# Moving the branch of an expert layer's overflow part from the end to behind the first expert

## The chip, the cores and the metric

One core of one Trainium2 chip runs the program. The metric is the device time of one execution in microseconds. The kernel before takes 1451.56 us (median of 3 runs, 1450.8 to 1453.4).

## The reference, cut to what matters

A decoder trunk of two layers on 256 tokens of width 1024. Each layer has a mixer of three kinds of heads, a feed-forward part and a gated input embedding; the first layer's feed-forward part is dense, the second's is a choice of two out of eight experts:

```
logits = t @ router;  top_val, top_idx = top_k(logits, 2);  gates = softmax(top_val)
for e in range(8):
    out = out + combine[:, e:e+1] * ((silu(t @ wg[e]) * (t @ wu[e])) @ wd[e])
h = h + out
h = h + sigmoid(rmsnorm(h) @ ple_gate) * (p @ ple_proj);   return rmsnorm(h)
```

Every expert has three float32 matrices of 1024 x 3584, 42 blocks of 1 MB; eight experts are 352 MB.

## The kernel before, in words

**Slots.** An expert's tokens are gathered into slots, multiplied, and added back into h. Expert 0 has 128 slots and is computed first, as a `Job`. The other seven are put in order of their number of tokens on the device; the three with fewest tokens get 64 slots each (`Halves`), the other four 128 (`Listed`). `ORDER` (L33) lists the places as they are worked on: 64, 128, 128, 64, 128, 128, 64 slots. Tokens past an expert's slots belong to the overflow part (`overflow`, L1181 to L1201): it loads the largest count into a register of every engine (L1183) and branches (L1184); only where some expert has too many tokens does a loop over all experts run (`Late`, two passes of a whole expert in its body). With the inputs used here the branch skips it.

**A cut.** An expert's 3584 columns are taken in cuts of 1024, 1024, 1024 and 512 (`run`, L1138). For a cut: `up` of the gate half, the transposes of the cut before (`turn`), `up` of the other half, `hidden` of the cut before, and `down` of the cut before. So the first cut of an expert stands ahead of the last `down` of the expert before it, and `scatter` (four adds into h, L1027) follows in the next steps. At the second cut of an expert the next one's rows are gathered and transposed (`prepare`), and the one after that is fetched by POOL (`fetch`, L1046).

**Arithmetic.** With 128 slots each block is split by ACT and DVE into a high part `whi` (L190) and a low part `wlo` (L191), and PE does 12 matmuls of 512 columns per block (L203). With 64 slots the blocks are used as they are, two blocks at a time in `up`, and the profile shows 8 matmul records of some 0.22 us per block.

**The ring.** All weight loads are issued by SP (`load`, L126), in the order of the program. A block goes into a buffer named raw. There are three pools: number 0 with 4 buffers, number 1 with 7, number 2 with 1. Unless a pool is named by `at`, `Ring.buffer` (L164) takes the one whose count of requests per buffer is lowest, and raises its count. The counts are kept by the program that writes the instructions, not by the chip, so they count what is written, run or not:

```
        def buffer(self, at=None):
            q = min(self.pools, key=lambda q: (q[2] + 1) / q[1]) if at is None else self.pools[at]
            q[2] += 1
            return q[0].tile([128, WMAX], FT, name="raw", tag="raw", bufs=q[1])
```

`Late` names pool 0 (L1036), and the last gate's weights name pool 1. A load waits until its buffer has been used up: with 128 slots when DVE has made `wlo`, with 64 when PE has done its matmuls.

**The end.** After the last expert's adds, `before_overflow` asks for the four blocks of the last gate (`ple_gate`, L656), then comes `overflow`, then `ple` (L662): h is transposed (L279), split (L230, L231), and multiplied with the gate's weights, which ACT and DVE scale and split (L195, L196); then the sigmoid, the last norm and the store. Nothing outside the branch's block is mixed with what is inside it, and no instruction crosses it.

Of the kernel before, what the change touches and what calls it, by code (L numbers as in the profile page):

```python
# [12 lines left out]
FR = mybir.dt.float32r  # L13
# [5 lines left out]
D = 1024  # L19
S = 256  # L20
NT = 2
KD = D // 128
# [75 lines left out]
def hymba_trunk(ctx: ExitStack, tc: tile.TileContext, A: dict, out: bass.AP, stop=None, dump=None):  # L98
# [14 lines left out]
    def aux():  # L113
        return psum.tile([128, 512], FT, name="aux", tag="aux")
# [10 lines left out]
    def load(t, src):  # L125
        nc.sync.dma_start(t, src)  # L126
        return t

    def const(name, p):
        lo, hi = _AT[name]  # L130
        C[name] = load(p.tile([128, hi - lo], FT, name="c_" + name), A["consts"][:, lo:hi])
        return C[name]
# [22 lines left out]
    class Ring:  # L155
        def __init__(self, p, raw, parts):
            self.p, self.parts = p, parts
            self.pools = [[p, raw, 0]]
# [70 lines left out]
    def split(hi, lo, src):  # L229
        ins = ACT.copy(hi, src)  # L230
        V.tensor_tensor(lo, src, hi.bitcast(FT), op=OP.subtract)  # L231
        return ins
# [654 lines left out]
        return xrow, slot, gate, rs, cmax_i, gates, places, who_i, slot_at, gate_at, caps, xd, rsd, rows_i  # L887


    def moe(ring, ep, slots, slots2, experts, routed, ready, before_overflow):  # L890
        xrow, slot, gate, rs, cmax_i, gates, places, who_i, slot_at, gate_at, caps, xd, rsd, rows_i = routed

        wg, wu, wd = A["moe_w_gate"][0], A["moe_w_up"][0], A["moe_w_down"][0]
# [6 lines left out]
        todo = []  # L900

        def step():
            if todo:
                todo.pop(0)()

        class Job:

            at = None
# [5 lines left out]
            def tiles(self):  # L914
                self.pe = ep.tile([128, NT, 128], FT, name="pe")
                self.pt = ep.tile([128, NT, 128], FR, name="pt")
                self.rs = ep.tile([128, 1], FT, name="rs_slot")

            def choose(self, names):
                for t in range(NT):  # L920
                    V.tensor_scalar(self.pe[:, t], names, self.col(t), None, op0=OP.is_equal)
# [19 lines left out]
            def prepare(self):  # L941

                self.tiles()
                xh, xl = (ep.tile([128, KD, 128], FR, name="xgh"), ep.tile([128, KD, 128], FR, name="xgl"))
                self.x = xh, xl

                def gather(k0):
                    ps = aux()
                    for j in range(4):
                        self.gathered(ps, j * 128, k0 + j, 128)  # L950
                    split(xh[:, k0:k0 + 4], xl[:, k0:k0 + 4], ps.rearrange("p (k n) -> p k n", k=4))

                return [lambda: self.choose(slots), lambda: gather(0), lambda: gather(4), self.scales, self.back]

            def unit(self, src, nk, n, pieces=1):
                return ring.unit(src, nk, n, pieces=pieces, halves=1, at=self.at)
# [77 lines left out]
        class Late(Job):  # L1034

            at = 0  # L1036

        class Listed(Job):

            names, n = slots, 128  # L1040
# [13 lines left out]
                PE.transpose(ps[:, at:at + self.n], self.xg[:self.n, k * 128:(k + 1) * 128], ident[:self.n, :self.n])  # L1054

            def prepare(self):
                xh, xl = (ep.tile([128, KD, 128], FR, name="xgh"), ep.tile([128, KD, 128], FR, name="xgl"))
                self.x = xh, xl

                def turn(k0):  # L1060
                    ps = aux()
                    for j in range(4):
                        self.turned(ps, j * 128, k0 + j)
                    split(xh[:, k0:k0 + 4], xl[:, k0:k0 + 4], ps.rearrange("p (k n) -> p k n", k=4))

                return [lambda: self.choose(self.names), lambda: turn(0), lambda: turn(4), self.back]

        class Halves(Listed):
# [5 lines left out]
            names, n = slots2, PCAP  # L1074
# [10 lines left out]
                return [lambda: self.choose(self.names), turn, self.back]  # L1085

            def unit(self, src, nk, n, pieces=1):
                return ring.fetch(src, nk, n, pieces)[0]

            def passes(self, os, x, ks, w, start, stop):  # L1090
                for n, o in enumerate(os):
# [43 lines left out]

        CUTS = [(c, min(1024, FE - c)) for c in range(0, FE, 1024)]

        def run(jobs, between=None):  # L1138

            steps = jobs[0].prepare()  # L1140
            for s in steps[:-1]:
                s()
            todo.append(steps[-1])
            if between:
                between()
            cuts = [(job, i) for job in range(len(jobs)) for i in range(len(CUTS))]
            back = None
            for cut in cuts + [None]:
                if cut:
                    job, (c0, n) = jobs[cut[0]], CUTS[cut[1]]  # L1150
                    pg = job.up(0, c0, n)
                if back:
                    pt = back[0].turn(back[3], back[2])
                if cut:
                    pu = job.up(1, c0, n)
                    with tc.issue_after(ring.split[0].ins):
                        job.gate_out(pg, n)
                if back:
                    with tc.issue_after(ring.split[0].ins), tc.issue_after(ring.split[1].ins):
                        hx = back[0].hidden(pt, back[2])  # L1160
                    us = back[0].down_units(back[1], back[2], 1 if cut else 2)
                if cut:
                    with tc.issue_after(ring.split[1].ins) if cut != cuts[-1] else nullcontext():
                        side = job.up_out(pu, n)
                if back:
                    back[0].down(back[1], hx, us)
                if cut:
                    back = (job, c0, n, side)
                    if cut[1] == 1 and cut[0] + 1 < len(jobs):
                        todo.extend(jobs[cut[0] + 1].prepare())  # L1170
                        if cut[0] + 2 < len(jobs):
                            todo.append(jobs[cut[0] + 2].fetch)
            while todo:
                step()

# [3 lines left out]
        se = ep.tile([128, NT, 2], FT, name="se", bufs=1)  # L1179

        def overflow():  # L1181
            V.memset(ei, 0.0)
            n_max = nc.values_load(cmax_i[0:1, 0:1], min_val=0, max_val=S + CAP - PCAP)  # L1183
            with tc.If(n_max > CAP):  # L1184
                xrow = ring.buffer(1)[:, :NT * D].rearrange("p (t d) -> p t d", t=NT)
                for t in range(NT):
                    load(xrow[:, t], xd[t * 128:(t + 1) * 128, :])
                for t in range(NT):
                    V.tensor_tensor(slot[:, t], slot[:, t], caps, op=OP.subtract)
                with tc.For_i(0, NE, 1) as e:  # L1190
                    V.tensor_scalar(hot, experts, ei, None, op0=OP.is_equal)
                    V.tensor_scalar(ei, ei, 1.0, None, op0=OP.add)
                    for t in range(NT):
                        for z, src in ((0, slot), (1, gate)):
                            hj = ep.tile([128, NE], FT, name="hj", bufs=2)
                            V.scalar_tensor_tensor(hj, hot, 1.0, src[:, t], op0=OP.mult, op1=OP.mult,
                                                   accum_out=se[:, t, z:z + 1])
                    for s0 in range(CAP, S + CAP - PCAP, 128):
                        sc = ep.tile([128, NT], FT, name="sc", bufs=2)
                        V.tensor_scalar(sc, se[:, :, 0], float(-s0), None, op0=OP.add)  # L1200
                        run([Late(lambda: e, lambda t: sc[:, t:t + 1], lambda t: se[:, t, 1:2], xrow)])  # L1201

        es = {}

# [7 lines left out]
        def between():  # L1212
            todo.append(know)
            todo.append(gates)

        jobs = ([Job(lambda: 0, lambda t: slot[:, t, 0:1], lambda t: gate[:, t, 0:1], xrow)]
                + [(Halves if j < NPACK else Listed)(j) for j in ORDER])
        run(jobs, between)
        before_overflow()
        overflow()  # L1220

    def store():
        for t in range(NT):
            nc.sync.dma_start(out[0, t * 128:(t + 1) * 128, :], h[:, t])

    ring = Ring(pool("ring"), 4, 3)
# [15 lines left out]
    with scoped("xt", 2, "right") as xp, scoped("xn", 2, "right") as xnp:  # L1242
# [47 lines left out]
        if stop == "mix1":  # L1290
# [4 lines left out]
        slots, below, experts, slots2, base, tok = [  # L1295
            const(n, pl) for n in ("slots", "below", "experts", "slots2", "base", "tok")]
# [15 lines left out]
        routed = routing(ring, pl, logits, g1, below, experts, base, tok, fill)  # L1312
    gates = []
    with scoped("moe", 2, "right") as ep, scoped("ringC", 1, "right") as rc:
        ring.widen(rc, 1)
        moe(ring, ep, slots, slots2, experts, routed, [first], lambda: gates.append(ple_gate(1, ring, 1)))
# [43 lines left out]
```

## Time and profile before

| | |
|---|---|
| median of 3 runs | 1451.56 us |
| profiled execution: time | 1452.36 us |
| its span, first to last instruction | 1450.6 us |
| mean granted TensorE clock in it | 0.992 |
| PE busy | 1398.5 us (96%) |
| DVE, ACT busy | 915.8 us (63%), 748.4 us (52%) |
| moved from HBM | 442.64 MB, 307 GB/s over the span |

The profile is that of one execution on the chip. Times count from the span's first instruction. PE is the matmul engine, PEld its weight loads, DVE, ACT, POOL and SP the other engines; a q behind an engine's name is its sequencer, which waits, branches and issues transfers. The DMA share is that of the 16 DMA engines. The expert layer begins near 500 us and ends at 1409 us.

### The profile page before, as it was taken

Reading aid. Unit: us, or ns where it says so; the run is one execution under the profiler, and the core shown is the slowest. Engines: PE = TensorE matmul, PEld = TensorE weight load, DVE = VectorE, ACT = ScalarE, POOL = GpSimd, SP = SyncE. Lnnn points to the kernel's source line nnn. Section 1 sums busy time; section 2 is a strip of 40 time slices with the busy share of each in tenths; the row PEclk is TensorE's granted clock in tenths of the full one; section 3 lists DMA queues with packets and bytes.
Section 4 is the critical chain, followed back from the end, with each engine's and each line's share of the span. In section 5 each row is a group of like instructions: output and inputs, shape, how many; then the busy total and the mean of one; then the engine's idle time right before and its main releaser. Section 6 shows DMA issues by size and latency. Waiting matters only on the chain. (4 is left out here: it accounts for less than half of the span.)

```text
span 1450.6 us, 19133 instructions
## 1 busy us (share of the span) xinstructions
PE 1398.5 (96%) x7330; PEld 1058.3 (73%) x7330; DVE 915.8 (63%) x1084; ACT 748.4 (52%) x874; POOL 69.0 (5%) x104
## 2 busy tenths in 40 slices
PE   8999999999999999999899999999999999999977
PEld 7987999997897887854378888864357888884426
DVE  6666555557766687831179898952158988882115
ACT  5455444447546566720167776741047767761006
POOL 0011000000001122000000000000000010000001
PEclk9999999999999999999999999999999999999998
DMA  8744555554634799999999999989999999999991
GB/s 287 207 145 138 176 194 183 183 195 148 223 117 148 194 307 366 403 408 409 401 409 399 402 408 409 385 338 382 402 408 409 389 408 409 402 376 356 371 363 45
DMA packets 168342, 446.09 MB, mean 308 GB/s; under 512 B 14449, under 2 KB 57713, under 8 KB 168242
## 3 DMA queue, kind: packets, MB, share of 16 engines
q1 hardware_dynamic: 166466, 440.83, 81.7%
q0 software_dynamic: 1776, 3.95, 1.2%
q8 instruction: 60, 0.98, 0.3%
q14 instruction: 40, 0.33, 0.1%
HBM read 442.64 MB, written 2.11 MB: 307 GB/s over the span
## 5 line engine op out<-in xcount | busy, mean ns | idle before, releaser
L191 DVE TENSOR_TENSOR wlo<-raw,whi 128x2048 fp32r<-128x2048 f32 (+2 forms) x348 | 638.3, 1865 | 188.9 <-ACT whi L190 187.0
L190 ACT CAST whi<-raw 128x2048 fp32r<-128x2048 f32 (+2 forms) x348 | 534.8, 1570 | 247.5 <-PE mm L203 117.4
L203 PE MATMUL mm<-whi,xgh 128*128 128x512 f32 x560 | 223.5, 399 | 4.5 <-ACT whi L190 4.5
L203 PE MATMUL mm<-whi,xgl 128*128 128x512 f32 x560 | 220.7, 394 | 0.5 <-DVE xgl L231 0.5
L203 PE MATMUL mm<-raw,xgp 128*64 128x512 f32 x672 | 160.7, 596 | 2.2 <-DMA raw<-in_moe_w_up_dram 2.2
L203 PE MATMUL mm<-wlo,xgh 128*128 128x512 f32 x560 | 155.0, 398 | 0.2 <-DVE wlo L191 0.2
L203 PE MATMUL mm<-xh,whi 128*128 128x256 f32 x512 | 129.3, 284 | 0.0
L203 PEld LDWEIGHTS mm<-whi,xgh 128*128 128x128 f32 x560 | 105.9, 189 | 31.3 <-ACT whi L190 6.3
L203 PE MATMUL mm<-xl,whi 128*128 128x256 f32 x512 | 128.5, 283 | 0.0
L203 PEld LDWEIGHTS mm<-raw,xgp 128*64 128x64 f32 x672 | 57.1, 136 | 92.8 <-issue 88.0
L203 PEld LDWEIGHTS mm<-whi,xgl 128*128 128x128 f32 x560 | 106.1, 189 | 23.7 <-DVE xgl L231 0.7
L203 PEld LDWEIGHTS mm<-wlo,xgh 128*128 128x128 f32 x560 | 103.8, 189 | 24.4 <-DVE wlo L191 1.9
L203 PE MATMUL aux<-whi,hxh 128*128 128x512 f32 x280 | 111.1, 397 | 7.7 <-ACT whi L190 7.7
L203 PE MATMUL mm<-whi,xh 128*128 128x512 f32 (+2 forms) x328 | 109.4, 349 | 3.2 <-ACT xh L230 3.2
L203 PE MATMUL mm<-whi,xl 128*128 128x512 f32 (+2 forms) x328 | 110.0, 349 | 0.0
L203 PE MATMUL aux<-whi,hxl 128*128 128x512 f32 x280 | 109.9, 393 | 0.0
L203 PEld LDWEIGHTS mm<-xh,whi 128*128 128x128 f32 x512 | 97.1, 190 | 1.6 <-issue 0.7
L203 PEld LDWEIGHTS mm<-xl,whi 128*128 128x128 f32 x512 | 97.3, 190 | 0.6
L203 PE MATMUL mm<-wlo,xh 128*128 128x512 f32 (+2 forms) x328 | 87.5, 347 | 0.1
L203 PE MATMUL aux<-raw,hxp 128*64 128x512 f32 x336 | 82.8, 597 | 1.8 <-DVE hxp L1133 0.9
L203 PE MATMUL mm<-xh,wlo 128*128 128x256 f32 x512 | 82.3, 281 | 0.0
L203 PE MATMUL aux<-wlo,hxh 128*128 128x512 f32 x280 | 78.6, 403 | 0.4 <-DVE wlo L191 0.4
(251 smaller groups left out, 1513.8 us busy)
## 6 DMA issues: line engine op xcount, KB each, us to landing
raw<-in_moe_w_gate_dram SPq DMA_DIRECT2D x112, 1024.0 KB, 18.1
raw<-in_moe_w_up_dram SPq DMA_DIRECT2D x112, 1024.0 KB, 15.0
raw<-in_moe_w_down_dram SPq DMA_DIRECT2D x110, 1024.0 KB, 16.2
raw<-in_w_in_dram SPq DMA_DIRECT2D x24, 1024.0 KB, 5.5
raw<-in_dense_w_gate_dram SPq DMA_DIRECT2D x11, 1024.0 KB, 5.5
raw<-in_dense_w_up_dram SPq DMA_DIRECT2D x11, 1024.0 KB, 5.4
raw<-in_dense_w_down_dram SPq DMA_DIRECT2D x11, 1024.0 KB, 4.9
raw<-in_w_out_dram SPq DMA_DIRECT2D x8, 1024.0 KB, 5.0
```

The source lines that it names most:

```text
L190: self.split = (ACT.copy(hi, v[:, k]), V.tensor_tensor(lo, v[:, k], hi.bitcast(FT), op=OP.subtract))
L191: V.tensor_tensor(lo, v[:, k], hi.bitcast(FT), op=OP.subtract))
L203: return PE.matmul(o, a, b, start=start, stop=stop, skip_group_check=True)
```

## The change

`overflow` is called between expert 0 and the second expert. `run` is split in two calls: the first does expert 0 alone, with the second expert's preparation in it (`later`); the second call does the other seven, with nothing to prepare for the first of these (`ready`). Expert 0 thus ends with its last `down` and its adds before the branch, with no cut of the second expert ahead of them. Before the branch, `begin(7)` asks for the first seven blocks of the second expert, all in pool 1; the eighth is asked for behind it. The third expert's `fetch` stands behind the branch. `Late` no longer allocates tiles of its own but takes those of one `like` job, and the overflow part's token rows go to pool 2.

```diff
+            def tiles(self):
+                self.pe, self.pt, self.rs, self.x = self.like.pe, self.like.pt, self.like.rs, self.like.x
...
             def unit(self, src, nk, n, pieces=1):
-                return ring.fetch(src, nk, n, pieces)[0]
+                return self.early.pop(0) if self.early else ring.fetch(src, nk, n, pieces)[0]
...
+            def begin(self, n):
+
+                self.early = [ring.fetch(rows((wg, wu)[i % 2], self.e(), i // 2 * 256, 256, slice(0, 1024)), 2, 1024,
+                                         at=1)[0] for i in range(n)]
...
-        def run(jobs, between=None):
-
-            steps = jobs[0].prepare()
-            for s in steps[:-1]:
-                s()
-            todo.append(steps[-1])
+        def run(jobs, between=None, ready=False, later=()):
+
+
+            if not ready:
+                steps = jobs[0].prepare()
...
             if between:
                 between()
+            line = [*jobs, *later]
...
-                xrow = ring.buffer(1)[:, :NT * D].rearrange("p (t d) -> p t d", t=NT)
+                xrow = ring.buffer(2)[:, :NT * D].rearrange("p (t d) -> p t d", t=NT)
...
-        run(jobs, between)
-        before_overflow()
+        run(jobs[:1], between, later=jobs[1:2])
+        jobs[1].begin(7)
+        halves = ring.split
         overflow()
+        ring.split = halves
+        run(jobs[1:], jobs[2].fetch, ready=True)
+        before_end()
```

## Rows read from the trace of the kernel before

**Rows 1.** The page: span.

```profile
span 1450.6 us, 19133 instructions
```

**Rows 2.** Windows by expert stage: engines' busy us (count), granted clock, DMA share, GB/s.

```profile
626.30:723.70 97.40, 88.97 (x396) 35.53 (x395) 16.35 (x24) 12.75 (x18) 1.89 (x2) 1.00 1.03 406
723.70:970.90 247.20, 246.50 (x1092) 196.53 (x1092) 211.13 (x128) 170.57 (x118) 6.39 (x4) 0.99 1.02 399
970.90:1063.30 92.40, 87.26 (x393) 35.69 (x392) 16.34 (x24) 12.74 (x18) 1.89 (x2) 1.00 0.97 377
1063.30:1309.20 245.90, 245.00 (x1090) 195.28 (x1090) 210.64 (x124) 170.40 (x118) 6.69 (x2) 1.00 1.02 400
```

**Rows 3.** Waits from 718 to 726 us: total, times, longest.

```profile
ACT whi L190 <- DMA raw<-in_moe_w_gate_dram: 19.6, 2, 19.0
...
PE mm L203 <- ACT whi L190: 2.4, 1, 2.4
```

**Rows 4.** Timeline of PE at the end: start, us, instruction, [idle before].

```profile
1399.88 4.17 PE L203 MATMUL aux<-raw,hxp 128*64 128x512 f32 x16 [0.94 <-DVE hxp L1133]
...
1406.72 0.40 PE L203 MATMUL aux<-yxl,pt 128*128 128x512 f32 x1
1413.63 0.66 PE L279 MATMUL aux<-ident,h 128*128 128x128 f32 x2 [6.52 <-PEq L1184]
1416.17 3.25 PE L279 MATMUL aux<-ident,h 128*128 128x128 f32 x14 [1.88 <-issue]
1419.07 0.78 PE L203 MATMUL mm<-whi,xh 128*128 128x512 f32 x1
```

**Rows 5.** Timeline of DVE at the end.

```profile
1405.99 2.77 DVE L1027 SCALAR_TENSOR_TENSOR h<-aux,gate_at,h 128x512 f32<-128x512 f32 x4
1414.20 1.41 DVE L196 SCALAR_TENSOR_TENSOR wlo<-raw,gcol,whi 128x512 fp32r<-128x512 f32 x2 [5.43 <-ACT whi L195]
1417.56 0.69 DVE L231 TENSOR_TENSOR xl<-aux,xh 128x512 fp32r<-128x512 f32 x1 [1.95 <-ACT xh L230]
...
1422.76 1.28 DVE L231 TENSOR_TENSOR xl<-aux,xh 128x512 fp32r<-128x512 f32 x2
```

**Rows 6.** The branch's line: duration ns min/median/max, first and last start us.

```profile
L1184 SPq EVENT_SEMAPHORE  x8: 17/17/17, 1407.4 to 1413.8; - x8
...
L1184 PEldq COMPARE_BRANCH  x1: 6602/6602/6602, 1406.6 to 1406.6; - x1
L1184 DVEq COMPARE_BRANCH  x1: 72/72/72, 1407.8 to 1407.8; - x1
...
L1184 DVEq EVENT_SEMAPHORE  x1: 21/21/21, 1413.0 to 1413.0; - x1
```

**Rows 7.** A window at the end, columns as in rows 2.

```profile
1412.00:1416.00 4.00, 0.66 (x2) 0.29 (x2) 1.41 (x2) 1.34 (x2) 0.00 (x0) 0.50 0.21 59
```

**Rows 8.** Timelines of DVE, PE and ACT where expert 0 ends.

```profile
619.08 2.29 DVE L191 TENSOR_TENSOR wlo<-raw,whi 128x2048 fp32r<-128x2048 f32 x1 [0.48 <-ACT whi L190]
...
626.26 7.09 PE L203 MATMUL mm<-raw,xgp 128*64 128x512 f32 x32
633.28 0.66 PE L994 MATMUL aux<-ident,sg 128*128 128x128 f32 x4
...
633.98 0.59 ACT L230 CAST hxh<-aux 128x512 fp32r<-128x512 f32 x1 [14.93 <-PE aux L994]
...
634.59 0.69 DVE L231 TENSOR_TENSOR hxl<-aux,hxh 128x512 fp32r<-128x512 f32 x1 [12.56 <-ACT hxh L230]
```

**Rows 9.** Timeline of SP: the last of ten requests there, all since 593.8 us.

```profile
617.14 2.25 SPq L126 DMA_DIRECT2D raw<-in_moe_w_down_dram  x1
```

**Rows 10.** Transfers, 600 to 626 us and of the page: KB each, us to landing.

```profile
raw<-in_moe_w_down_dram SPq DMA_DIRECT2D x2, 1024.0 KB, 18.1
...
raw<-in_w_out_dram SPq DMA_DIRECT2D x8, 1024.0 KB, 5.0
```

**Rows 11.** Timeline of SP in the second 64-row stage.

```profile
998.47 0.37 SPq L126 DMA_DIRECT2D raw<-in_moe_w_gate_dram  x1
```

More of the change, by code (lines that the diff above doesn't have):

```diff
@@ L887, in routing, with moe @@
         return xrow, slot, gate, rs, cmax_i, gates, places, who_i, slot_at, gate_at, caps, xd, rsd, rows_i
-    def moe(ring, ep, slots, slots2, experts, routed, ready, before_overflow):
+    def moe(ring, ep, slots, slots2, experts, routed, ready, before_end):
         xrow, slot, gate, rs, cmax_i, gates, places, who_i, slot_at, gate_at, caps, xd, rsd, rows_i = routed
@@ L917, in tiles, with room @@
                 self.rs = ep.tile([128, 1], FT, name="rs_slot")
+            def room(self):
+                self.x = (ep.tile([128, KD, 128], FR, name="xgh"), ep.tile([128, KD, 128], FR, name="xgl"))
+                return self.x
             def choose(self, names):
@@ L943, in prepare @@
                 self.tiles()
-                xh, xl = (ep.tile([128, KD, 128], FR, name="xgh"), ep.tile([128, KD, 128], FR, name="xgl"))
-                self.x = xh, xl
+                xh, xl = self.room()
                 def gather(k0):
@@ L1036, in moe, with __init__, room @@
             at = 0
+            def __init__(self, like, e, col, gcol):
+                super().__init__(e, col, gcol, like.xrow)
+                self.like = like
+            def tiles(self):
+                self.pe, self.pt, self.rs, self.x = self.like.pe, self.like.pt, self.like.rs, self.like.x
+            def room(self):
+                return self.x
         class Listed(Job):
@@ L1056, in prepare @@
             def prepare(self):
-                xh, xl = (ep.tile([128, KD, 128], FR, name="xgh"), ep.tile([128, KD, 128], FR, name="xgl"))
-                self.x = xh, xl
+                xh, xl = self.room()
                 def turn(k0):
@@ L1087, in unit @@
             def unit(self, src, nk, n, pieces=1):
-                return ring.fetch(src, nk, n, pieces)[0]
+                return self.early.pop(0) if self.early else ring.fetch(src, nk, n, pieces)[0]
+            early = ()
+            def begin(self, n):
+                self.early = [ring.fetch(rows((wg, wu)[i % 2], self.e(), i // 2 * 256, 256, slice(0, 1024)), 2, 1024,
+                                         at=1)[0] for i in range(n)]
             def passes(self, os, x, ks, w, start, stop):
@@ L1136, in moe @@
         CUTS = [(c, min(1024, FE - c)) for c in range(0, FE, 1024)]
-        def run(jobs, between=None):
-            steps = jobs[0].prepare()
-            for s in steps[:-1]:
-                s()
-            todo.append(steps[-1])
+        def run(jobs, between=None, ready=False, later=()):
+            if not ready:
+                steps = jobs[0].prepare()
+                for s in steps[:-1]:
+                    s()
+                todo.append(steps[-1])
             if between:
                 between()
+            line = [*jobs, *later]
             cuts = [(job, i) for job in range(len(jobs)) for i in range(len(CUTS))]
@@ L1168, in run @@
                     back = (job, c0, n, side)
[L1169 to L1172, printed above, removed]
+                    if cut[1] == 1 and cut[0] + 1 < len(line):
+                        todo.extend(line[cut[0] + 1].prepare())
+                        if cut[0] + 2 < len(line):
+                            todo.append(line[cut[0] + 2].fetch)
             while todo:
@@ L1184, in overflow @@
             with tc.If(n_max > CAP):
-                xrow = ring.buffer(1)[:, :NT * D].rearrange("p (t d) -> p t d", t=NT)
+                xrow = ring.buffer(2)[:, :NT * D].rearrange("p (t d) -> p t d", t=NT)
                 for t in range(NT):
                     load(xrow[:, t], xd[t * 128:(t + 1) * 128, :])
+                like = Job(None, None, None, xrow)
+                like.tiles()
+                like.room()
                 for t in range(NT):
@@ L1200, in overflow @@
                         V.tensor_scalar(sc, se[:, :, 0], float(-s0), None, op0=OP.add)
-                        run([Late(lambda: e, lambda t: sc[:, t:t + 1], lambda t: se[:, t, 1:2], xrow)])
+                        run([Late(like, lambda: e, lambda t: sc[:, t:t + 1], lambda t: se[:, t, 1:2])])
         es = {}
```

## The prediction

> **What bounds the kernel now.** Read first the page and the stage table. The profiled execution took 1452.4 us, of which 1450.6 are the span [rows 1]; the median of the runs is 1451.56, 0.8 below it. From 626 us on the seven experts of the list run in three kinds of stage [rows 2]: a 64-row expert, two 128-row experts, a 64-row one, two 128-row ones, a 64-row one. In the 128-row pairs PE is busy for 246.5 of 247.2 us, and weights flow at 399 to 400 GB/s: PE sets the pace. In the first 64-row stage PE is busy for 89.0 of 97.4 us and the DMA share is 1.03: weights set the pace, at 406 GB/s, or 2.6 us for a block of 1 MB. That this stage ends on a transfer is seen in the waits at 718 to 726: ACT's split for the next expert waits 19.0 us for its first block [rows 3]. So the chain alternates: transfers in the stage behind the seam, PE in the next, and so on. What delays transfers at 626 to 724 is not caught up later, since the PE-bound pair simply starts later.
>
> Then read the end. PE's last matmul of the last expert ends at 1404.05, its last add into h at 1407.12; the next work on PE starts at 1413.63, stops again for 1.88 us, and the first matmul of the gate product comes at 1419.07 [rows 4]. DVE has the last h at 1408.76 [rows 5]. Between them stands the branch: PE's own compare-and-branch takes 6602 ns, DVE goes on 5.2 us after its own, and SP works off eight semaphores, from 1407.4 to 1413.8 [rows 6]. [...]
>
> **The change, part by part.**
>
> *The end loses the branch.* Transposes of h can follow each add, so the first matmul could start near 1409 instead of 1419.1: 10 us at best. DVE keeps some of it back. Before, it made the first half's eight low parts and four differences from 1414.20 to 1424.0 with a 1.95 us hole [rows 5]; they are 8 x 0.70 + 4 x 0.65 = 8.2 us, and put right behind the last add (1408.8) they end at 1417.0, 7.0 us earlier. I take 7.5 us, between 5.5 (the order on DVE is as bad as before) and 10. [...] SP's semaphores go from the end too; the four gate blocks are asked for ahead, as now, and stay beside the last expert's work.
>
> *The seam gets the branch.* What is issued there, with the branch not taken: a memset, a register load and a branch on each engine, and SP's eight semaphores. I read the last of these (1413.8) as SP waiting until what it has asked for has landed. Behind SP's wait stand all further weight loads; behind PE's wait the next expert's first products. POOL only has the third expert's gathers behind it, which are used after 660 us: nothing.
>
> First PE. The last matmul before the next expert now ends at 626.3 [rows 8]. In the changed order expert 0's last cut follows at once: transpose, copy and difference are 0.66 + 0.59 + 0.69 [rows 8], so 628.2; two blocks at 2.94 us (247.2 us for the 84 of a pair [rows 2]), 5.9, so 634.1; scatter as at the end, 1404.05 to 1407.12 [rows 4], 3.1, so 637.2. The branch costs 6.5 us there (1407.12 to 1413.63 [rows 4]); DVE's 5.2 us bounds it from below, PE's own 6.6 from above. PE is back at 643.7.
>
> Now the transfers. SP's queue before: eight blocks of the next expert and expert 0's last two have been asked for by 617.1 [rows 9], and land 18.1 us after their request [rows 10], so the tenth lands near 635.2. With seven of the eight asked ahead, the ninth lands one block earlier, at 632.6. All seven must fit: their buffers fall free as expert 0 is split (the last split but two ends at 621.4 [rows 8]), soon enough. So the seven blocks do cover SP's own stop.
>
> They don't cover PE's. The seven go into the pool of seven buffers and fill it. The part that is skipped is still written out once when the program is built: two passes of 42 weight blocks each ask the pool of four by name, and each request raises that pool's count by one. The next buffer is chosen by the lowest count per buffer. 84 / 4 puts the pool of four 21 rounds ahead, and the pool of seven has to pass 147 blocks before it is chosen again: through the next 3 to 4 experts the ring has 7 + 1 buffers, not 12. The eighth block therefore waits until PE has used up the first two blocks: 3.5 us at full clock (7.09 us for four blocks [rows 8]), 7.0 at the clock level seen after the pause [rows 7]; I take 6.0. So 649.7, plus 0.2 to issue and 5.0 from request to landing on an empty queue [rows 10]: 654.9. The same ten blocks landed by 635.2: **19.7 us lost** by the transfers. Bounds: 13.3 (full clock -2.5, branch 5.2 us -1.3, the one-buffer pool's block sent ahead of the waiting one -2.6) to 22.3 (half clock all through +1.0, ACT copying before it splits +1.6). PE has no excuse to end later: from 649.7 it needs 38 blocks at 1.77 us and some 8 us of pauses, 725, and the transfers end near 742. The stage therefore ends 19.7 us later, and the PE-bound pair starts by that much later.
>
> *Eight buffers at the second 64-row expert.* In that stage PE has caught up with up to twelve blocks in hand; loads are asked for only as buffers fall free (a request takes 0.37 us there [rows 11], against 2.25 where the queue is full [rows 9]), and the stage moves 377 GB/s [rows 2]. With eight in hand four blocks more have to come in its course: 4 x 2.6 = 10.4 us at most, nothing if PE hides it. I replayed the stage with each request at the release of the eighth block before it instead of the twelfth, 5 us to the first landing and 2.6 between blocks: the next expert's first block lands 7.0 us later. I take 7.0. By the third 64-row expert the pool of four is back in turn and no loss is left. The 128-row pairs are PE-bound, with blocks to spare: nothing, and if that cover is gone, see rival two.
>
> **Sum:** 1452.4 + 19.7 + 7.0 - 7.5 = 1471.6 against the profiled execution, and 0.8 less against the median: **1470.8 us**.
>
> [...]
>
> **The rivals.**
> 1. *The cover holds: faster.* If the eighth block finds a free buffer as soon as SP is past its semaphores (the skipped part's requests don't steer the choice, or the four buffers come first), transfers stop only from 632.6 for some 2.4 us, and no stage runs on eight buffers: 1452.4 + 2.4 - 7.5 - 0.8 = 1446.5. It decides where the loss at the seam and behind it stays under 7.5 us. For it: seven blocks, 18 us, are just what SP's pause needs. Against it: the count in the code. 0.10.
> 2. *Eight buffers starve the 128-row pair as well.* If PE then waits at each of eight cuts as it does at the start of the pair (2.4 us [rows 3]), 19 us more: 1490. Against it: there transfers are faster than PE and blocks are in hand. 0.05.
> 3. *Seam and end cancel.* Half of the loss is caught up in the PE-bound pair (0.7 us of its 247 are idle, so I see no room), 1452. 0.04.
> The forecast has the rest, 0.81.
>
> **How the numbers follow.** The forecast's terms at their ends give 1452.4 + 13.3 + 0 - 10 - 0.8 = 1454.9 and 1452.4 + 22.3 + 10.4 - 5.5 - 0.8 = 1478.8; not all ends come together, and with a little of rival two above, the range is 1456 to 1481. It leaves out most of rivals one and two, 0.15. A change within 0.2% (2.9 us) cannot be told from none here: faster 0.10, same 0.04, slower 0.86.
>
> **What would show it.** Right: in the second expert's start a hole of 15 to 20 us in the transfers after some seven blocks; the request for the eighth only after PE's first two blocks; PE idle for some 6.5 us before it at a falling clock; the first PE-bound pair as long as before but 19 us later; the second 64-row stage some 7 us longer, the third unchanged; at the end transposes right behind the adds, and a tail 7 us shorter. Wrong: transfers without a hole, or loads that go on while PE still pauses; a pair of 128-row experts that is longer than 248 us; a tail that is not shorter.

## The result and the profile after

The changed kernel takes 1468.84 us (median of 4 runs, 1466.8 to 1469.9) beside 1451.56 us for the kernel before on the same chip (three runs, 1450.8 to 1453.4; a fourth took 1483.63 us, 2.3% above the fastest, and is left out as slow): **ratio 1.0117, 95% interval 1.0103 to 1.0132, so about 1.2% slower**. Forecast: 1470.8, within 1456 to 1481. The profiled execution took 1469.9 us, 17.5 more than that of before.

First the page's span, to be held against [rows 1]:

```profile
span 1468.1 us, 19134 instructions
```

Then the windows by stage, with the seam cut finer (columns as in [rows 2]: window and length, busy us and count of PE, PEld, DVE, ACT, POOL, granted clock, DMA share, GB/s):

```profile
626.00:632.00 6.00, 5.33 (x25) 3.86 (x24) 1.72 (x2) 0.59 (x1) 0.00 (x0) 1.00 0.52 210
632.00:640.00 8.00, 4.06 (x16) 2.44 (x14) 4.05 (x6) 1.07 (x2) 0.00 (x0) 1.00 0.01 4
640.00:645.00 5.00, 4.53 (x14) 1.76 (x16) 0.88 (x4) 0.00 (x0) 1.04 (x1) 0.66 0.03 8
645.00:650.00 5.00, 5.00 (x26) 1.97 (x24) 0.00 (x0) 0.00 (x0) 0.00 (x0) 1.00 0.62 202
640.40:740.40 100.00, 87.41 (x358) 30.85 (x358) 7.97 (x18) 7.49 (x13) 2.93 (x3) 0.98 0.96 378
740.40:987.40 247.00, 246.25 (x1090) 196.38 (x1091) 211.09 (x128) 170.61 (x119) 6.38 (x4) 0.99 1.00 383
987.40:1090.00 102.60, 91.72 (x393) 36.05 (x392) 16.33 (x24) 12.76 (x18) 1.89 (x2) 1.00 0.97 382
1090.00:1335.70 245.70, 244.80 (x1090) 195.33 (x1090) 210.59 (x124) 170.64 (x118) 4.49 (x2) 1.00 1.02 401
...
1430.40:1468.10 37.70, 27.68 (x145) 22.26 (x144) 25.33 (x40) 23.87 (x48) 5.25 (x13) 0.94 0.31 114
```

Three places differ. **The seam:** from 632 to 645 us the DMA engines stand still (share 0.01 and 0.03), and the first 128-row pair starts at 740.46, not 723.69: 16.8 us lost. **The second 64-row stage** takes 102.6 us, not 92.4 [rows 2]: 10.2 lost. In it 382 GB/s x 102.6 us = 39.2 MB arrive, before 377 x 92.4 = 34.8: 4.4 MB more, four blocks that had not come ahead. **The tail** from the last `down` to the end of the span takes 37.7 us; before, 1404.05 to 1450.6, so 46.5: 8.8 won. The pairs stay at 247.0 and 245.7 us, the third 64-row stage at 94.7 (before 94.9). Together 16.8 + 10.2 - 8.8 = 18.2, against a span longer by 17.5.

SP's timeline at the seam and its largest wait from 618 to 660 us (total, times, longest) show who keeps the transfers:

```profile
621.53 0.37 SPq L126 DMA_DIRECT2D raw<-in_moe_w_up_dram  x1
624.26 0.37 SPq L126 DMA_DIRECT2D raw<-in_moe_w_gate_dram  x1
645.82 0.39 SPq L126 DMA_DIRECT2D raw<-in_moe_w_up_dram  x1
...
SPq L126 <- PE mm L203: 23.1, 5, 14.5
```

The seventh early block is asked for at 624.26, the eighth at 645.82, after a wait of 14.5 us that ends with a matmul: it had to have a buffer that the second expert's own first blocks were in. The branch's line (now L1206) and PE's timeline at the seam and at the end:

```profile
L1206 SPq EVENT_SEMAPHORE  x8: 17/17/17, 630.1 to 630.8; - x8
...
L1206 SPq COMPARE_BRANCH  x1: 50/50/50, 625.0 to 625.0; - x1
L1206 ACTq COMPARE_BRANCH  x1: 50/50/50, 634.2 to 634.2; - x1
...
L1206 PEldq COMPARE_BRANCH  x1: 3327/3327/3327, 636.3 to 636.3; - x1
L1206 DVEq COMPARE_BRANCH  x1: 72/72/72, 637.4 to 637.4; - x1
...
L1206 DVEq EVENT_SEMAPHORE  x1: 21/21/21, 640.4 to 640.4; - x1
```

```profile
636.34 0.40 PE L203 MATMUL aux<-yxl,pt 128*128 128x512 f32 x1
640.47 2.24 PE L203 MATMUL mm<-raw,xgp 128*64 128x512 f32 x6 [3.74 <-DVEq L1206]
...
1433.09 0.40 PE L203 MATMUL aux<-yxl,pt 128*128 128x512 f32 x1
1433.33 1.19 PE L279 MATMUL aux<-ident,h 128*128 128x128 f32 x8
1434.60 0.50 PE L203 MATMUL mm<-whi,xh 128*128 128x512 f32 x1
```

SP is through at 630.8, PE stands for 3.74 us and goes on at 640.47, and the eighth request comes only 5.35 us after that. At the end the transposes follow the last add without a pause, where [rows 4] has 6.52 and 1.88 us of idleness. The block of the eighth request lands at 650.91; the kernel before had the same number of blocks landed at 635.28.

### The profile page after: what moved, and what is told of

Its sections match the earlier page's. It is cut to its first block, busy times and chain, and to the rows that moved or that the text cites. A ratio compares the mean times of both kernels' runs of the same rounds, so it can differ in the third digit from the quotient of the medians.

```text
span 1468.1 us, 19134 instructions
## 1 busy us (share of the span) xinstructions
PE 1408.4 (96%) x7330; PEld 1058.1 (72%) x7330; DVE 915.5 (62%) x1084; ACT 748.7 (51%) x874; POOL 68.3 (5%) x104
## 4 chain that ended last, share of the span: by engine, by line
PE 46%; DMA 7%; issue 1%; DVE 1%; ACT 1%; POOL 0%; SPq 0%; POOLq 0%; ACTq 0%
PE mm L203 30%; PE aux L203 15%; DMA raw<-in_moe_w_up_dram 5%; DMA raw<-in_moe_w_gate_dram 2%; PE aux L997 1%; ACT whi L190 1%; PE aux L1067 0%; DVE wlo L191 0%; DVE h L1030 0%; ACT yxh L230 0%; ACT sq L248 0%; DVE h L257 0%; DVE xn L1358 0%; DVE ple_sg L690 0%; DVE wlo L196 0%
## 5 line engine op out<-in xcount | busy, mean ns | idle before, releaser
L203 PE MATMUL mm<-raw,xgp 128*64 128x512 f32 x672 | 171.4, 603 | 17.5 <-DMA raw<-in_moe_w_up_dram 10.3
L1140 DVE TENSOR_SCALAR sg<-mm,rs_slot 128x512 f32<-128x512 f32 x12 | 9.0, 750 | 113.4 <-PE mm L203 113.4
## 6 DMA issues: line engine op xcount, KB each, us to landing
raw<-in_moe_w_up_dram SPq DMA_DIRECT2D x112, 1024.0 KB, 13.2
```

The lines of the kernel that those rows point to most:

```text
L203: return PE.matmul(o, a, b, start=start, stop=stop, skip_group_check=True)
L1140: V.tensor_scalar(sg[:, HALF[z]], ps[z], self.rs, None, op0=OP.mult)
```

## The experiments

All times below are medians; A, B and C are read from PE's timeline in the profile of each run. A: first matmul of expert 0 to the first of the first 128-row pair. B: first matmul of the second 64-row expert to the first of the next pair. C: last `down` to the end of the span. Each ratio is to runs of the kernel before on the same chip in the same session. e3, e4, e5 and e9 leave out the overflow part together with its branch; its result is not needed for these inputs.

| kernel | us | ratio to before [95%] | A | B | C |
|---|---|---|---|---|---|
| before | 1450.3 to 1451.6 | 1 | 216.9 | 94.6 | 46.5 |
| after | 1468.84 | 1.0117 [1.0103, 1.0132] | 233.5 | 104.7 | 37.7 |
| e1_counts | 1454.66 | 1.0025 [1.0015, 1.0035] | 229.2 | 95.8 | 37.7 |
| e2_ring8 | 1467.26 | 1.0124 [1.0107, 1.0141] | 218.6 | 104.8 | 46.6 |
| e3_nobranch_skew | 1458.50 | 1.0055 [1.0038, 1.0072] | 221.5 | 104.8 | 37.3 |
| e4_end_nobranch | 1438.87 | 0.9922 [0.9905, 0.9939] | 215.1 | 94.9 | 37.4 |
| e5_nobranch | 1445.48 | 0.9965 [0.9953, 0.9978] | 219.7 | 95.8 | 37.3 |
| e6_ten | 1456.23 | 1.0043 [1.0026, 1.0060] | 228.5 | 94.6 | 37.7 |
| e7_none_ahead | 1469.02 | 1.0135 [1.0116, 1.0153] | 232.2 | 104.8 | 37.7 |
| e8_ten_mixed | 1456.83 | 1.0035 [1.0022, 1.0048] | 230.4 | 94.6 | 37.7 |
| e9_nobranch_order | 1440.16 | 0.9924 [0.9909, 0.9938] | 214.7 | 95.6 | 37.3 |
| e10_turn | 1447.89 | 0.9979 [0.9968, 0.9989] | 221.9 | 94.8 | 37.7 |

The theory to be tested: the loss comes from the counts that the skipped part leaves behind, and from the branch; the rivals give it to one of them alone, or to the order of the blocks.

**e4_end_nobranch: what the branch costs at the end.** The kernel before, without the overflow part.

```diff
-        overflow()
```

> The kernel before without the overflow part and its branch, which this leaves out; nothing is moved. Theory: all that the end gains comes from the branch being gone there: 8.9 us, 1443.6, with the stages up to the last add unchanged. Rival (part of the gain at the end comes from the order of the loads or from the later experts): 1446 to 1452.

PE's timeline at the end:

```profile
1402.70 0.40 PE L203 MATMUL aux<-yxl,pt 128*128 128x512 f32 x1
1402.94 1.20 PE L279 MATMUL aux<-ident,h 128*128 128x128 f32 x8
1404.27 0.50 PE L203 MATMUL mm<-whi,xh 128*128 128x512 f32 x1
```

The tail is 9.1 us shorter, as in the changed kernel (8.8): that gain is the branch's absence and nothing else. The time is below the 1443.6 us that were expected: the other 4.0 us of the 13.1 by which the span is shorter are spread over the stages ahead of the end (A 1.8, the pairs 2.3 of it). They go with the granted clock: over the span it was 0.992 in the kernel before and 0.998 in e4. Whether the missing branch raised the clock is not shown; the changed kernel, with no branch at its end either, has 0.994, and like the kernel before 0.99 in the first pair and 0.98 in the last 64-row stage.

**e2_ring8: the counts alone.** The kernel before, branch at the end, with the pool of four set 84 requests ahead where the second expert begins.

```diff
+                    if cut == (1, 0):
+                        ring.pools[0][2] += 84
```

> The kernel before, branch at its end, with the count of the pool of four raised by 84 at the second expert's first cut: a ring of eight for the next experts and nothing else. Theory: the first 64-row stage is unchanged, the second is 10 us longer (102 for 92), the 128-row pairs are unchanged: 1452.5 + 10 = 1462.5. Rival one (eight buffers cost nothing, the longer stage comes from the moved branch): 1452.5. Rival two (the first 64-row stage loses by the eight buffers too, not by the pause): 1470 or more.

The windows of the two 64-row stages:

```profile
623.80:727.50 103.70, 92.99 (x395) 37.00 (x394) 16.32 (x23) 12.74 (x18) 1.89 (x2) 0.98 0.97 381
...
974.20:1076.40 102.20, 90.98 (x393) 36.10 (x389) 16.37 (x24) 12.74 (x18) 1.89 (x2) 1.00 0.97 382
```

B is 104.8, as after: a count, with no load and no calculation added or moved by hand, costs 10.2 us there. The time missed its expectation (1462.5) and lies between it and rival two: A is 1.7 us longer too, which the expectation didn't have, and 2.1 us of the first pair's later start (727.52) were lost ahead of expert 0.

**e1_counts: the change with the counts put back.**

```diff
+        counts = [q[2] for q in ring.pools]
         overflow()
+        for q, n in zip(ring.pools, counts):
+            q[2] = n
```

> The changed kernel, with the ring's counts put back behind the overflow part to what they were ahead of it, so that the pool of four comes in turn again. Theory (the counts make the loss): the second 64-row stage is back at 92 us (10 us less), and the eighth block no longer waits for PE's first two blocks. If a buffer of the pool of four counts as free at once, the third expert starts near 727; if it counts as used by the skipped part until DVE is past the branch, near 734. The time is then 1468.8 - 10.2 - 6 to 14, that is 1444 to 1453. Rival (the pause of the engines makes the loss, whatever the counts): 1468.8, with the second 64-row stage at 102 us.

SP's timeline at the eighth request, its wait there, and the window of the second 64-row stage:

```profile
624.04 0.37 SPq L126 DMA_DIRECT2D raw<-in_moe_w_gate_dram  x1
640.25 0.39 SPq L126 DMA_DIRECT2D raw<-in_moe_w_up_dram  x1
...
SPq L126 <- DVEq L1206: 9.2, 1, 9.2
...
983.10:1076.50 93.40, 88.27 (x392) 36.72 (x388) 16.32 (x23) 12.73 (x18) 1.88 (x2) 0.98 0.95 373
```

Three lines of Python take back 14.2 us (1468.84 to 1454.66): 8.9 in B, 4.3 in A. Against the kernels before of their own sessions it is 1.0117 to 1.0025, some 13 us. The time is just above the expected 1444 to 1453: the seam still loses. The eighth block may now have a buffer of the pool of four, but that pool is used inside the branch's block, and the request waits 9.2 us, until DVE is past the branch. It goes out at 640.25 where SP was through at 630.4.

**e7_none_ahead: the change without its seven early requests.**

```diff
-        jobs[1].begin(7)
+        jobs[1].begin(0)
```

> The changed kernel with no block asked for ahead of the branch; the counts stay as they are there. Theory (SP is past the branch long before PE, and the pool of seven is free for it by then, so the same seven blocks come from behind the branch, in time for PE): a short hole of 2 to 8 us near 613, but the eighth block still waits for PE's first two, and the time is that of the changed kernel, 1469, within 3 us. Rival (the seven blocks ahead are what keeps the loss small; a request behind the branch waits for PE or DVE to be past it): the first block comes only at 640, the loss at the seam grows by 10 us or more, 1480.

SP's branch events and requests:

```profile
L1206 SPq EVENT_SEMAPHORE  x8: 17/17/17, 607.2 to 614.9; - x8
...
599.50 0.77 SPq L126 DMA_DIRECT2D raw<-in_moe_w_down_dram  x1
615.22 0.42 SPq L126 DMA_DIRECT2D raw<-in_moe_w_gate_dram  x1
...
623.21 0.37 SPq L126 DMA_DIRECT2D raw<-in_moe_w_gate_dram  x1
644.97 0.37 SPq L126 DMA_DIRECT2D raw<-in_moe_w_up_dram  x1
```

The same time as after, as expected: the early requests are worth nothing that can be seen. SP stands until expert 0's last block has landed, at 614.8, then asks for seven blocks while the other engines still work ahead of the branch; the eighth waits as before. So here the request behind the branch into a pool that the block doesn't use went out 0.3 us after SP's last event (615.22 after 614.9), and the one into a pool that it does use (e1) waited 9.2 us, for the engines.

**e3_nobranch_skew and e5_nobranch: the change without the branch,** with the counts as if the part were there, and without.

```diff
-        overflow()
+        ring.pools[0][2] += 84
+        ring.pools[2][2] += 1
```

> The changed kernel without the overflow part and its branch, which this leaves out, but with the counts raised as it raises them (84 and 1). PE has no pause between expert 0 and the second. Theory (the eighth block waits for PE's first two): PE starts the second expert 3.7 us earlier and at full clock, so the loss at the seam falls from 16.8 to about 11 us and does not vanish; the second 64-row stage stays at 102 us: 1463. Rival (the branch itself makes the hole in the transfers): no loss at the seam, 1452.

e5 has only the first of these three lines.

> The changed kernel without the overflow part and its branch, which this leaves out, and without its effect on the counts: what is left of the change is that expert 0 ends before the second expert begins, and the seven blocks ahead. Theory: the transfers have no hole, because the eighth block finds one of the pool of four; the third expert starts within 3 us of the kernel before, the second 64-row stage is at 92 to 95 us, the end is 9 us shorter: 1439 to 1443. Rival (expert 0's end without the next expert beside it costs by itself): the third expert starts 5 us or more later, 1445 or more.

In both, PE is not kept from the second expert: without a branch its first matmuls again stand among expert 0's last ones (the timeline of e9 below shows it). In e3 SP asks for the seventh block at 622.87 and for the eighth at 636.69, again behind the second expert's first matmuls; A is 12.0 us shorter than after, so with these counts the branch, with the end of expert 0 that it forces ahead of it, is worth 12.0 at the seam. e3's time is 4.5 us under the expected 1463, because its loss at the seam (4.6 in A) is smaller than the expected 11. e5 has neither branch nor raised counts, and still loses 4.6 us in A against e4; its 1445.48 us miss the expected 1439 to 1443 and reach the rival's time. SP's timeline of e5:

```profile
624.16 2.06 SPq L126 DMA_DIRECT2D raw<-in_moe_w_up_dram  x1
634.68 0.37 SPq L126 DMA_DIRECT2D raw<-in_moe_w_gate_dram  x1
647.78 0.37 SPq L126 DMA_DIRECT2D raw<-in_moe_w_up_dram  x1
648.36 0.37 SPq L126 DMA_DIRECT2D raw<-in_moe_w_gate_dram  x1
```

One request stands from 635.1 to 647.8, though there are twelve buffers. New theory: seven blocks bunched in one pool put the buffers out of the order in which they come free, and SP's queue waits at one that is late with free ones behind it.

**e9_nobranch_order: e5 with the early blocks dealt over the pools by the counts.**

```diff
-                                         at=1)[0] for i in range(n)]
+                                         at=None)[0] for i in range(n)]
```

> The kernel of e5_nobranch (the changed kernel without the overflow part and its branch, no count raised), with the seven early blocks dealt over the pools by the counts, as all other blocks, and not all in the pool of seven. Theory (bunched in one pool they are asked for out of the order in which buffers come free, and that alone costs the 4.2 us by which e5_nobranch's first pair starts later than e4_end_nobranch's 723.08): first pair at 723 to 724.5, no landing gap over 4 us between 620 and 660, time 1440 to 1442 us. Rival (finishing expert 0 ahead of the next expert's blocks costs it, whichever pool they are in): first pair near 727.2 and 1445.5 us, as e5_nobranch.

The window of the first 64-row stage, 406 GB/s as in [rows 2]:

```profile
624.40:723.30 98.90, 90.58 (x391) 35.55 (x390) 12.06 (x23) 9.04 (x16) 1.89 (x2) 1.00 1.03 406
```

A is 214.7, as in e4: the order was the whole of e5's loss, 5.0 us. What e9 doesn't show is what finishing expert 0 ahead of the next expert costs. The program is written in that order, but PE's timeline has the second expert's first matmuls more than 12 us ahead of expert 0's last add:

```profile
624.40 1.07 PE L203 MATMUL mm<-raw,xgp 128*64 128x512 f32 x2
...
637.10 0.40 PE L203 MATMUL aux<-yxl,pt 128*128 128x512 f32 x1
```

Of the kernels here only those with the branch between the two keep them apart (in after 636.34 and 640.47), so none has that order alone.

**e6_ten, e8_ten_mixed, e10_turn: can the seam be covered?** All have e1's restored counts. The overflow part works in the pool of one, with its rows in one buffer of the pool of four, so that ten blocks can be asked for ahead: in e6 seven in one pool, then three in the other.

```diff
-            at = 0
+            at = 2
...
-                xrow = ring.buffer(2)[:, :NT * D].rearrange("p (t d) -> p t d", t=NT)
+                xrow = ring.buffer(0)[:, :NT * D].rearrange("p (t d) -> p t d", t=NT)
...
-        jobs[1].begin(7)
+        jobs[1].begin(10)
```

> The changed kernel with the counts put back, the overflow part's own blocks in the pool of one, its rows in one buffer of the pool of four, and ten blocks asked for ahead of the branch in the other ten buffers. Theory (a block behind the branch waits for a buffer: those that the skipped part uses come free when DVE is past the branch, at 640 us, the others when PE has used them up): ten blocks last until about 638, the eleventh and twelfth are asked for at 640, so the hole is some 5 us instead of 19, and the third expert starts 5 us later than in the kernel before instead of 17; no loss at the second 64-row stage; 1451 + 5 - 9 = 1447. Rival (what counts is PE's pause, not the buffers): as with the counts put back alone, 1454.7.

A miss: the first pair starts at 735.11, in e1 at 735.75. Ten blocks are there by 638.6, but then one request stands until 654.15 and another until 660.98. Once e5 had been read as an effect of the order, e8 dealt the ten over the two pools in the order of use.

```diff
-                                         at=1 if i < 7 else 0)[0] for i in range(n)]
+                                         at=(1, 0, 1, 1, 0, 1, 1, 0, 1, 1)[i])[0] for i in range(n)]
```

> The kernel of e6_ten, with its ten early blocks dealt over the pool of seven and the pool of four in the order in which the matmuls will use them, where e6_ten asked for seven in one pool and then three in the other. Theory (e6_ten failed because buffers came free in another order than they are asked for, which made gaps of 4.95, 6.4 and 4.5 us between landings after the eleventh block): the only hole left is the one from the tenth landing, near 638.6, to the eleventh, near 645.2, so the first 128-row pair starts near 728 in place of 735.1, the second 64-row stage stays at 94 to 96 us, and the time is 1448 to 1450.5 us, level with the kernel before or just under it. Rival (the gaps of e6_ten are the engines' own pace after the pause, not the order of the buffers): first pair near 735, 1456 us as e6_ten.

A miss again, and the time that the rival gave, but not for its reason. SP's timeline of e8:

```profile
651.59 0.37 SPq L126 DMA_DIRECT2D raw<-in_moe_w_gate_dram  x1
665.32 0.37 SPq L126 DMA_DIRECT2D raw<-in_moe_w_up_dram  x1
665.88 2.42 SPq L126 DMA_DIRECT2D raw<-in_moe_w_down_dram  x4
```

The ten early blocks had raised the counts of two pools only, so by the counts the pool of one looked underused; it was chosen for the eleventh block and soon again for the sixteenth, which then stood for 13.2 us behind matmuls. The trace doesn't name the buffers; that this count is the cause rests on e10, which changes it alone.

```diff
             q[2] = n
+        ring.pools[2][2] += 0.7
```

> The kernel of e8_ten_mixed with 0.7 added to the count of the pool of one buffer, so that the eleventh block still takes that buffer and the sixteenth no longer does. In e8_ten_mixed the sixteenth request stood at 665.3 until the matmuls were through with the eleventh block, with free buffers of the other pools behind it in the queue, and made a landing gap of 9.81 us where 2.56 is the pace. Theory (a buffer that is asked for before its turn stops the whole queue): that gap goes, which gives back up to 7.2 us; the first 128-row pair starts 91 to 94 us after the second expert's first matmul (97.6 in e8_ten_mixed, 94.9 in e6_ten), and the time is 1449 to 1453 us. Rival (the pace after the pause is set by the engines): 95 us or more for that stage, 1456 us again.

The windows of the first 64-row stage, of the pair behind it, and of the tail:

```profile
640.20:728.70 88.50, 81.22 (x358) 29.14 (x358) 8.01 (x18) 7.60 (x13) 2.92 (x3) 0.97 1.01 392
728.70:975.20 246.50, 245.58 (x1092) 195.43 (x1094) 211.09 (x128) 170.59 (x118) 6.38 (x4) 1.00 1.02 401
...
1408.70:1446.40 37.70, 27.67 (x144) 22.27 (x144) 25.32 (x40) 23.87 (x48) 5.25 (x13) 0.93 0.31 116
```

The first pair starts at 728.73, 5.0 us later than before, against 8.8 won in the tail: 1447.89 us, ratio 0.9979 [0.9968, 0.9989]. With the branch at the seam this is the fastest, 0.2% below the kernel before and just under what was expected (1449 to 1453). Without a branch anywhere e4 and e9 come to 1439 to 1440.

## Why the prediction was right, and where its sizes were off

It forecast the right sign by the right chain, and each term has its measurement.

- **The seam: 19.7 forecast, 16.8 measured** (740.46 - 723.69). Expert 0's own steps held: last add's matmul 636.74 for 637.2. The term mis-sized is the pause: PE stood 3.74 us, not 6.5, and came back at 640.47 for 643.7. That step took the pause from the end of the kernel; at the seam it is 3.6 to 3.9 us (after, e1, e7, e10), at the end 6.3 (e2) and 6.5 (before). Both the lower bound (5.2, from DVE) and the value were too high. The first two blocks took 5.35 us for 6.0 (granted clock 0.66 from 640 to 645), so the eighth was asked for at 645.82 for 649.7 and landed at 650.91 for 654.9, 5.09 us after its request where 5.0 and 0.2 were taken; the 0.2 was the author's estimate, which no row shows. By that landing 15.6 us are lost; the last 1.1 of the 16.8 came later in the stage, which the prediction didn't have.
- **The eight buffers: 7.0 forecast, 10.2 measured,** close to the upper bound of 10.4 that the prediction worked out as four blocks of 2.6 us. Its replay let PE hide part of the four; PE hid none. e2 shows the same term with the branch still at the end, and e1 shows it gone with the counts put back.
- **The end: -7.5 forecast, -8.8 measured.** DVE kept back less than was thought: its timeline there has the last add and right behind it the first low part of h.

```profile
1432.36 2.77 DVE L1030 SCALAR_TENSOR_TENSOR h<-aux,gate_at,h 128x512 f32<-128x512 f32 x4
1435.04 0.68 DVE L231 TENSOR_TENSOR xl<-aux,xh 128x512 fp32r<-128x512 f32 x1
```

So the three errors, -2.9, +3.2 and -1.3, nearly cancel, and the total is nearer than its terms deserve.

- **"So the seven blocks do cover SP's own stop"** holds (SP's events end at 630.8, the last packet of the early blocks at 630.1), but the sentence credits the cover with a worth it doesn't have: e7 has none ahead and the same time. SP's stop is over long before PE's in either case.
- **Rival one** was right in half of its mechanism. Put the counts right and 14.2 us come back, but not down to the rival's 1446.5: its other condition, that the eighth block finds a free buffer as soon as SP is past its semaphores, fails in e1, since the pools used inside the block stay busy until DVE is past the branch (the wait of 9.2 us). The prediction saw no such wait. Rival two (starved pairs) is out: 247.0 us for 247.2. So is rival three, since a pair of that length catches nothing up.
- What the seam's A consists of, by the kernels that differ in one thing: 214.7 without branch and in order (e9); +5.0 for the seven bunched in one pool (e5); +1.8 for the counts (e3); +12.0 for the branch and the order on PE that it forces (after). The terms are not independent: with the counts right the branch costs 229.2 - 219.7 = 9.5, and with ten blocks ahead in the right order 221.9 - 214.7 = 7.2 (e10 against e9, which differ in the early blocks too).

## What to carry to other kernels

A branch that is never taken still has a price, here about 9 us at the end and 7 to 12 in the middle, and in the middle it is paid through the transfers: what decides is which buffers the next loads may have while the engines pass it. State that is kept while the program is written (a ring's counts) also counts code that the chip skips; save and restore it around such code. With one queue and several pools, ask for buffers in the order in which they come free, since one request that is ahead of its turn stops all that are behind it (13.2 us in e8): two such slips cost 5.0 (e5 against e9) and 8.5 us (A of e8 against e10) here.

## What was not expected of the hardware

PE's compare-and-branch lasted 3327 to 3707 ns at the seam (after, e1, e7, e10), and 6602 and 6462 ns at the end (before, e2), for nearly the same skipped code. The traces show where the difference arises. While PE's branch lasts, one instruction transfer of 16 KB passes on the queue q8. The DMA queues (packets, MB, share of the 16 engines) in before from 1406.6 to 1410.2 us, the branch's first 3.6 us, and from 1410.2 to 1411.6; then in after from 637.2 to 638.3, with nothing on any queue in the 0.9 us of the branch ahead of it:

```profile
q1 hardware_dynamic: 692, 1.38, 103.8%
...
q1 hardware_dynamic: 133, 0.25, 51.7%
...
q8 instruction: 1, 0.02, 5.4%
...
q8 instruction: 1, 0.02, 5.4%
```

At the end this transfer starts 3.6 us into the branch, when the last gate's blocks are nearly in; at the seam, where the weight transfers have all but stopped, it starts 1.0 us into it. From the transfer's end to that of the branch it is 1.7 us in before and 1.4 in after. So 2.6 of the 3.3 us between the two places pass before this transfer starts. That it waits behind the weights is what the rows suggest; no run took those blocks away, so it is not shown.

The pause is not the same on every engine, nor in both places: ACT had its next event 0.6 us behind its branch at the seam (634.2 to 634.8), 5.4 at the end (1404.6 to 1410.0).

SP's part of the branch follows the landing of its own transfers, not the other engines: its last event comes at 614.9 in e7, where the last packet is in by 614.8, and at 630.8 in after, where it is in at 630.1; PE and DVE are past the branch only at 639.0 and 639.5 in e7, at 639.7 and 640.4 in after.
